# A hybrid layer on one Trainium2 core: the second gate's product cut in two, its row spread through memory, and one expert's weights asked for first

## The chip, the cores and the metric

The kernel runs on one core of one Trainium2 chip. The metric is the device time of one launch in microseconds (us). Engines are TensorE (PE, products; PEld is its weight load), VectorE (DVE), ScalarE (ACT), GpSimd (POOL) and SyncE (SP, which here issues most transfers). Each engine works through its own instructions in order; semaphores tie them together. Sixteen DMA engines move the data between the memory of the chip (DRAM) and the on-chip buffers.

## The reference

One transformer layer for 256 tokens of width 1024, in float32. A conditioning vector c gives six modulation rows:

```
mod = (silu_c @ w_ada + b_ada).reshape(bsz, 6, d)
sh1, sc1, g1, sh2, sc2, g2 = ...
u = modulate(x, sh1, sc1)
mix = hybrid_mixer(u, ...)                 # RG-LRU half, attention half, w_out
x = layernorm(ALPHA * x + g1 * mix, ln1_g, ln1_b)
u2 = modulate(x, sh2, sc2)
ffn = hierarchical_moe(u2, ...)            # 32 experts, 2 per token, chosen by a router
x = layernorm(ALPHA * x + g2 * ffn, ln2_g, ln2_b)
```

The change touches the last of these rows, g2 (called v=5 in the kernel), which multiplies what the experts give.

## The kernel before, in words

The tokens are handled as two halves of 128 (i = 0 and 1). The kernel is one long straight program: a tile framework puts in the semaphores, but the order of the instructions on every engine is the order of the source (`manual_schedule`), so a line that stands earlier in the source is earlier on its engine.

The stages, in order: the modulation rows and the input projection (to about 100 us); attention, output product and first layer norm, together with the router, mixed by hand (100 to 165 us); then the experts (165 to 290 us) and the last layer norm.

Weights come in loads of 1024 KB, two per call of `load` (line 229), issued by SP. SP goes through its list in order; a load waits until the buffer that it overwrites is free. `arena` has six slots of 16 KB per partition; `last`, `misc` and `fifth` are three more buffers of that size. `last` takes the place of the buffers of the input projection; `misc` holds small things and the softmax tiles until `pv_mm(1, 1)`; `fifth` takes the place of `mT` and `lnb` when the second half's `x2_of` has read them.

Six experts are expected to be busy, from the router's bias alone. `early_experts` ranks them on DVE and leaves their row numbers in `eos`. `statics((e, part), ...)` (line 859) issues the loads of expert e: part 0 and 1 are w1 and w3 (into `place[e][0]`), part 2 is w2. The first call also makes SP read six numbers of `eos` into registers (line 856). Experts 0 to 3 are used by the first `products` (line 1212, `ph0`), experts 4 and 5 by later units. The other experts are only known when the router is done; `bring_all` loads them (lines 1166 and 1169) as the buffers come free.

Gate v of the modulation is a product over 1024 inputs in two halves: `V1[v, q]` holds the weights of half q, `vec_mm(v, q, pa2)` (line 590) makes 16 calls that add to the bank `pa2`. For g2 the bias rows are added by four small products, ACT copies the result to `row3` (four rows of 256, at partitions 0, 32, 64 and 96), and four products with a broadcast column of the identity spread it over all partitions into the bank `acc[1]`; ACT copies it to `g2b`. The first reader of `g2b` is line 1362, which scales the first experts' output rows.

The row for the second modulation already goes through DRAM: `mod2_out` writes `mod2d`, `mod2_in` reads it back as `mod2p` (SP, lines 660 and 664). `constants()` (lines 942 to 946) reads `mod2p[:, 1]`.

For token half i, `bn_end` (line 885) makes the mean and the reciprocal standard deviation: DVE adds epsilon (line 274), POOL takes the power -0.5 (line 275). `logits` needs that value in its second instruction (line 933); `top` picks the experts; then PE ranks the tokens (lines 1127 to 1131), DVE makes slots, and `early_rows(1)` on PE (line 1070) gathers the tokens for the early experts. `norms` (line 1050 on POOL, line 1051 on ACT) makes the rows that it gathers.

Of the kernel before, what the change touches and what calls it, by code (L numbers as in the profile page):

```python
# [10 lines left out]
F32 = mybir.dt.float32  # L11
# [4 lines left out]
AF = mybir.ActivationFunctionType  # L16
# [5 lines left out]
S, D = 256, 1024  # L22
# [125 lines left out]
def layer(ctx: ExitStack, tc: tile.TileContext, at_a, at_b, x, w_ada, b_ada, w_in, w_out, w1, w3, w2,  # L148
          pack_a, pack_b, w_gate, rb, ln, out, dbg=None):
    nc = tc.nc  # L150
    te, ve, se, ge, sy = nc.tensor, nc.vector, nc.scalar, nc.gpsimd, nc.sync
# [7 lines left out]
    drm = ctx.enter_context(tc.tile_pool(name="drm", bufs=1, space=DRAM))  # L159
# [15 lines left out]
    misc = front.enter_context(tc.tile_pool(name="mis", bufs=1, reuse_waits="tile")).tile([128, 4096], F32, name="misc")  # L175
# [18 lines left out]
    def bank(pool=None):  # L194
        turn[0] += 1
        return (pool or (psx, psp)[turn[0] % 2]).tile([128, 512], F32, name="b")

    def abank():
        return psa.tile([128, 512], F32, name="a")
# [6 lines left out]
    brows = misc[:, 2048:3072].rearrange("p (g n) -> p g n", g=2)  # L206

    def A(name):
        o, w = at_a[name]
        return pka[:, o:o + w]  # L210

    def K(name, rows=128):
        o, w = at_b[name]
        return pkb[:rows, o:o + w]
# [9 lines left out]
    def load(s, src):  # L224
        n, w = src.shape[1:]
        t = (slot(s) if isinstance(s, int) else s).rearrange("p (k n) -> p k n", k=n)
        for h in range(2):
            q = slice(h * n // 2, (h + 1) * n // 2)
            sy.dma_start(t[:, q], src[:, q])  # L229
        return t  # L230

    def load_vec(v, q, s):
        return load(s, ada[:, 4 * q:4 * q + 4, v * D:(v + 1) * D])
# [16 lines left out]
    V1 = {}  # L250
# [7 lines left out]
    ident = A("ident")  # L258
# [23 lines left out]
    cd = ch.tile([128, KD, 32], F32, name="cd")  # L282
# [94 lines left out]
    def vec_cols(v):  # L377
        pa = abank()
        for k in range(KD):
            for j in range(4):  # L380
                te.matmul(pa[32 * j:32 * j + 32, 0:256], cd[:, k], V1[v, k // 4][:, k % 4, j * 256:(j + 1) * 256],
                          start=(k == 0), stop=(k == KD - 1), skip_group_check=True, tile_position=(0, 32 * j))
        r = tmp.tile([128, 256], F32, name="row", bufs=1)
        ve.tensor_copy(r, pa[:, 0:256])
        p = bank(psx)
        for s in range(2):
            te.matmul(p[:, s:8:2], r[:, s * 128:(s + 1) * 128], sel4, start=True, stop=True)
        return p[:, 0:8]
# [69 lines left out]
    p = vec_cols(0)  # L458
# [20 lines left out]
    for k in range(KD):  # L479
        j = k % 4  # L480
        te.matmul(pb[32 * j:32 * j + 32], shd[:, k], W["x"][:, k], start=(k < 4), stop=(k >= 4), skip_group_check=True,  # L481
                  tile_position=(0, 32 * j))
# [57 lines left out]
    def early_experts():  # L540
        row, rank = prior[:, :NE], prior[:, NE:2 * NE]
        ve.tensor_scalar(stat, rank, RS - 0.5, 32.0, op0=OP.is_gt, op1=OP.mult)
        ve.scalar_tensor_tensor(stat, rank, RS + NS - 0.5, stat, op0=OP.is_lt, op1=OP.mult)
        ve.tensor_scalar(e32, rank, 32.0, -32.0 * RS - 128.0 * UA, op0=OP.mult, op1=OP.add)


        ve.tensor_scalar(row, rank, 0.5, 64.0, op0=OP.is_lt, op1=OP.mult)
        ve.tensor_add(cap, stat, row)
        ve.tensor_scalar(row, rank, 1.5, 64.0, op0=OP.is_lt, op1=OP.mult)
        ve.tensor_add(cap, cap, row)  # L550
        ve.scalar_tensor_tensor(row, rank, float(NS + 1), row, op0=OP.add, op1=OP.mult)
        ve.tensor_scalar(v512, rank, 2.0, 2.0 * (1 - RS), op0=OP.mult, op1=OP.add)
        ve.tensor_mul(v512, v512, stat)
        ve.tensor_add(v512, v512, row)
        ve.tensor_scalar(v512, v512, 8.0, None, op0=OP.mult)
        ve.tensor_scalar(sel[:, 3], cap, -1.0, None, op0=OP.mult)
        ve.tensor_copy(dat[:, :, 0], K("foff"))
        eid = ch.tile([128, NS + 2], F32, name="eids")
        for j in range(NS + 2):
            ve.scalar_tensor_tensor(row, rank, float(RS + j if j < NS else j - NS), K("e"), op0=OP.is_equal, op1=OP.mult,  # L560
                                    accum_out=eid[:, j:j + 1])
        ve.tensor_scalar(eos, eid, 128.0, None, op0=OP.mult)
# [23 lines left out]
    def vec_mm(v, q, pt):  # L586
        o = (v - 4) * 256
        for k in range(4):
            for j in range(4):
                te.matmul(pt[32 * j:32 * j + 32, o:o + 256], cd[:, 4 * q + k], V1[v, q][:, k, j * 256:(j + 1) * 256],  # L590
                          start=(q + k == 0), stop=(v == 4 and q == 1 and k == 3), skip_group_check=True,
                          tile_position=(0, 32 * j))

    def vec_rows(v, pt):
# [147 lines left out]
    def pt(i, b):  # L742
        sn, at = AT[i, b]
        n, w = sn.shape[1:]
        p = bank()
        for c in range(n):
            for j in range(w // 128):
                o = (j * n + c) * 128
                te.transpose(p[:, o:o + 128], sn[:, c, j * 128:(j + 1) * 128], ident)
        t = misc[:, 3072 + at:3584 + at]  # L750
        se.activation(t, p, AF.Copy)
        AT[i, b] = t
# [55 lines left out]
    def base(i, h):  # L808
        p = wo_mm(i, h, 0)
        sl = slice(h * 512, (h + 1) * 512)  # L810
        t = tmp.tile([128, 512], F32, name="s")
        ve.scalar_tensor_tensor(t, p, rl[:, i:i + 1], g1b[:, sl], op0=OP.mult, op1=OP.mult)
        ve.scalar_tensor_tensor(xt[:, i, sl], xt[:, i, sl], ALPHA, t, op0=OP.mult, op1=OP.add)
# [24 lines left out]
    early.close()  # L838
    late = ctx.enter_context(tc.tile_pool(name="lat", bufs=1, reuse_waits="tile"))
    last = late.tile([128, 4096], F32, name="last")  # L840
    V1[5, 1] = load_vec(5, 1, last)
    merge = ctx.enter_context(ExitStack())
    merge_pool = merge.enter_context(tc.tile_pool(name="mrg", bufs=1, reuse_waits="tile"))
    mT = merge_pool.tile([128, 8, 256], F32, name="mT")
# [4 lines left out]
    pa2 = abank()  # L849
# [4 lines left out]
    def load_static(e, part):  # L854
        if not srows:
            srows.extend(nc.values_load(eos[0:1, j:j + 1], engines=[mybir.EngineType.SP], min_val=0, max_val=(NE - 1) * 128)
                         for j in range(NS + 2))
        src = ex[("w1", "w3", "w2")[part]][bass.ds(srows[e], 128)]
        sy.dma_start(place[e][1] if part == 2 else place[e][0][:, part * 2048:(part + 1) * 2048], src)
# [3 lines left out]
    def statics(*parts):  # L863
        for e, part in parts:
            load_static(e, part)
# [51 lines left out]
    def raw_mm(i, zT):  # L917
        p = bank(psp)
        for k in range(KD):
            te.matmul(p[:, 0:36], zT[:, k], wsh[:, k, 0:36], start=(k == 0), stop=(k == KD - 1))  # L920
        return p
# [19 lines left out]
    def constants():  # L941
        ve.tensor_tensor(wsh[:, :, 36:72], wr, cols_of(mod2p[:, 1]), op=OP.mult)
        ve.tensor_tensor(wsh[:, :, 0:36], wsh[:, :, 36:72], cols_of(A("lcol")[:, 0:8]), op=OP.mult)
        ve.tensor_tensor(wsh[:, :, 72:108], wsh[:, :, 36:72], cols_of(A("lcol")[:, 8:16]), op=OP.mult)

        ve.tensor_reduce(wsum[:, 0:108], wsh.rearrange("p k e -> p e k"), axis=AX.X, op=OP.add)
# [37 lines left out]
    norm(0, 1)  # L984
    pt(0, 0)
    early_experts()
    vec_mm(4, 0, pa2)
    statics((0, 0), (0, 1))
    pt(0, 1)
# [25 lines left out]
    scores(1, 3)  # L1015
    constants()
    vec_mm(5, 0, pa2)
    statics((2, 0), (2, 1))
    pv_mm(1, 0)
    vec_mm(5, 1, pa2)  # L1020
    for j in range(4):
        te.matmul(pa2[32 * j:32 * j + 32, 256:512], ident[:, 32 * j:32 * j + 1].to_broadcast([128, 32]), brows[:, 1, 256:512],
                  start=False, stop=True, skip_group_check=True, tile_position=(0, 32 * j))
    row3 = cd.rearrange("p k n -> p (k n)")
    se.activation(row3, pa2[:, 256:512], AF.Copy)
    statics((3, 0), (3, 1))
    pt(1, 2)
    norm(1, 3)
    base(1, 0)
# [10 lines left out]
    logits(0, t0, st0)  # L1040
    top(0)
    base(1, 1)
    statics((4, 0), (4, 1), (0, 2), (1, 2))
    rms_cols(row, ra[:, 1:2], psp)
    bs = [wo_mm(1, 0, 1, psx)]
    nmr = ch.tile([128, 2], F32, name="nmr")
# [50 lines left out]
    acc = [[accp.tile([128, 512], F32, name=f"acc{i}{h}") for h in range(2)] for i in range(2)]  # L1097
# [3 lines left out]

    acc_init(0, 0)
    pl1 = raw_mm(1, zT1)
    g2b = mox.tile([128, D], F32, name="g2b")
    for j in range(4):
        te.matmul(acc[1][j // 2][:, j % 2 * 256:j % 2 * 256 + 256], ident[:, 32 * j:32 * j + 1].to_broadcast([128, 128]), row3,
                  start=True, stop=True)
    acc_init(0, 1)
    for h in range(2):
        se.activation(g2b[:, h * 512:(h + 1) * 512], acc[1][h], AF.Copy)  # L1110
    x2_of(1, *lnst[1])
    st1 = bn(1, x2[:, 1])
    st1 = bn_end(*st1)
# [2 lines left out]
    merge.close()  # L1116
    fifth = ctx.enter_context(tc.tile_pool(name="fif", bufs=1, reuse_waits="tile")).tile([128, 4096], F32, name="fifth")
    place.append((fifth, w2_at[5]))
    statics((4, 2), (5, 0), (5, 1), (5, 2))
    logits(1, t1, st1)  # L1120
    top(1)
    dump("lg", lg)
# [3 lines left out]
    p = bank(psp)  # L1126
# [66 lines left out]
    for k in range(KD):  # L1193
        q, sc, sh = pgs[k // 4][:, k % 4 * 128:k % 4 * 128 + 128], mod2p[:, 1, k:k + 1], mod2p[:, 0, k:k + 1]
# [541 lines left out]
```

## Time and profile before

| | |
|---|---|
| time, median of 3 runs | 307.26 us (307.08 to 308.35) |
| the profiled execution | 307.51 us, its span 305.7 us |
| PE busy | 278.0 us (91%) |
| DVE busy | 181.7 us (59%) |
| ACT busy | 108.2 us (35%) |
| POOL busy | 23.6 us (8%) |
| moved by the DMA engines | 112.22 MB, mean 367 GB/s |
| mean granted PE clock | 0.988 of full speed |

The span runs from the first to the last instruction of one execution; the time also holds what lies around it. Busy times are of one engine and overlap with those of the others. A chain of waits is followed back from the last instruction: at each step to what released it, or else to the instruction ahead of it on its engine. In rows, `L590` is line 590; `b<-arena,mT` reads "writes b, reads arena and mT"; `x32` counts instructions (one float32 product in the source is two of them).

### The profile page before, as it was taken

How to read it: one execution, taken by the hardware profiler on the slowest of the kernel's cores; microseconds unless marked ns; L12 is line 12 of the kernel's file. 1: busy time of each engine (PE TensorE's matmuls, PEld its weight loads, DVE VectorE, ACT ScalarE, POOL GpSimd, SP SyncE). 2: the span in 40 equal slices, each digit the busy share in tenths (PEclk: the TensorE clock that was granted, in tenths of full speed). 3: DMA queues.
4: the chain of work that ended last, by engine and by line, in shares of the span. 5: the costliest groups of instructions: out<-in, count | busy, mean ns of one | idle time of the engine just before them, and what ended most of it. 6: DMA issues, size and time to landing. Idle time of an engine off the chain costs nothing.

```text
span 305.7 us, 6096 instructions
## 1 busy us (share of the span) xinstructions
PE 278.0 (91%) x2344; PEld 185.1 (61%) x2344; DVE 181.7 (59%) x442; ACT 108.2 (35%) x229; POOL 23.6 (8%) x62
## 2 busy tenths in 40 slices
PE   0699889999999999999988969999999999998980
PEld 0579649797957745457475656667546754664430
DVE  2675167937686796689698964264426343434281
ACT  1233068868937542043417341113111312121110
POOL 0100613000010000000110200000000000400000
PEclk9999979999999999999999999999999999999997
DMA  7999999999999699699969999999999999999404
GB/s 271 387 391 408 393 396 404 385 395 420 411 409 407 248 416 421 235 402 378 323 263 364 364 416 427 418 421 419 423 423 415 421 419 420 421 414 404 177 3 148
DMA packets 26163, 112.22 MB, mean 367 GB/s; under 512 B 2253, under 2 KB 3586, under 8 KB 17420
## 3 DMA queue, kind: packets, MB, share of 16 engines
q1 hardware_dynamic: 25712, 111.26, 91.7%
q10 hardware_dynamic: 348, 0.47, 0.4%
q8 instruction: 20, 0.33, 0.4%
q14 instruction: 19, 0.16, 0.2%
q0 software_dynamic: 64, 0.01, 0.0%
HBM read 110.51 MB, written 1.22 MB: 365 GB/s over the span
## 4 chain that ended last, share of the span: by engine, by line
PE 63%; DMA 13%; DVE 12%; SPq 6%; ACT 2%; issue 2%; DVEq 0%; ACTq 0%
PE m L1212 14%; PE b L430 12%; PE m L1350 8%; PE b L804 7%; DMA arena<-in_w 6%; DMA arena<-in_w_in 6%; SPq L229 4%; PE b L779 4%; PE m L1288 4%; PE acc L1311 3%; PE a L578 2%; PE a L590 2%; PE acc L1387 1%; PE b L481 1%; PE b L617 1%
## 5 line engine op out<-in xcount | busy, mean ns | idle before, releaser
L430 PEld LDWEIGHTS b<-ul,w 128*128 128x128 f32 x384 | 46.6, 192 | 5.0 <-ACT ul L470 1.6
L430 PE MATMUL b<-ul,w 128*128 128x256 f32 x384 | 48.4, 286 | 0.5 <-ACT w L410 0.5
L1212 PE MATMUL m<-arena,xg 128*64 128x256 f32 (+1 forms) x288 | 36.1, 380 | 1.0 <-DMA arena<-in_w 1.0
L408 DVE TENSOR_TENSOR w<-arena,w 128x512 fp32r<-128x512 f32 x32 | 21.9, 700 | 16.1 <-ACT w L407 16.1
L1350 PE MATMUL m<-arena,hT 128*32 128x512 f32 (+2 forms) x184 | 29.1, 596 | 1.6 <-ACT hT L1341 1.6
L804 PE MATMUL b<-arena,mT 128*128 128x512 f32 x64 | 29.0, 601 | 0.0
L1212 PEld LDWEIGHTS m<-arena,xg 128*64 128x64 f32 (+1 forms) x288 | 21.1, 125 | 9.9 <-DMA arena<-in_w 1.7
L407 ACT ACTIVATE w<-arena 128x512 fp32r<-128x512 f32 x32 | 19.5, 625 | 13.9 <-DMA arena<-in_w_in 7.1
L1212 PE MATMUL m<-fifth,xg 128*32 128x256 f32 (+1 forms) x96 | 21.5, 380 | 0.0
L1212 PE MATMUL m<-misc,xg 128*32 128x256 f32 (+1 forms) x160 | 21.4, 380 | 0.0
L1362 DVE SCALAR_TENSOR_TENSOR ys<-m,ws,g2b 128x256 f32<-128x256 f32 (+1 forms) x21 | 11.4, 570 | 16.0 <-PE m L1350 15.8
L1363 ACT ACTIVATE yh<-ys 128x256 fp32r<-128x256 f32 (+1 forms) x21 | 10.0, 488 | 27.0 <-DVE ys L1362 26.9
L1331 DVE TENSOR_TENSOR hh<-hh,m 128x256 f32<-128x256 f32 x7 | 3.0, 422 | 27.9 <-ACT hh L1330 27.9
L804 PEld LDWEIGHTS b<-arena,mT 128*128 128x128 f32 x64 | 11.6, 191 | 13.0 <-issue 12.7
L1350 PEld LDWEIGHTS m<-arena,hT 128*32 128x32 f32 (+2 forms) x184 | 8.6, 120 | 17.8 <-issue 12.7
L1330 ACT ACTIVATE hh<-m 128x256 f32<-128x256 f32 x7 | 2.7, 385 | 41.1 <-PE m L1212 41.1
L1288 PE MATMUL m<-oh,xb 128*128 128x256 f32 (+1 forms) x64 | 15.4, 281 | 1.3 <-DVE oh L1279 1.3
L1288 PE MATMUL m<-oh,xa 128*128 128x256 f32 (+1 forms) x64 | 15.4, 282 | 0.0
L1212 PEld LDWEIGHTS m<-misc,xg 128*32 128x32 f32 (+1 forms) x160 | 13.3, 126 | 1.6 <-issue 0.8
L1212 PE MATMUL m<-last,xg 128*32 128x256 f32 x64 | 14.2, 380 | 0.0
L728 ACT ACTIVATE s<-s,z 128x128 f32<-128x128 f32 (+1 forms) x16 | 7.1, 449 | 18.3 <-DVE z L726 18.3
L305 PE MATMUL b<-pka,nx 128*128 128x128 f32 x16 | 3.9, 428 | 10.3 <-DVE nx L303 10.3
(321 smaller groups left out, 501.2 us busy)
## 6 DMA issues: line engine op xcount, KB each, us to landing
arena<-in_w SPq DMA_DIRECT2D x41, 1024.0 KB, 11.9
arena<-in_w_ada SPq DMA_DIRECT2D x22, 1024.0 KB, 13.9
arena<-in_w_in SPq DMA_DIRECT2D x10, 1024.0 KB, 15.1
last<-in_w SPq DMA_DIRECT2D x6, 1024.0 KB, 12.2
misc<-in_w SPq DMA_DIRECT2D x6, 1024.0 KB, 13.3
fifth<-in_w SPq DMA_DIRECT2D x6, 1024.0 KB, 13.0
arena<-in_w_out SPq DMA_DIRECT2D x4, 1024.0 KB, 8.8
arena<-in_w SPq DMA_DIRECT2D x8, 512.0 KB, 12.7
```

The costliest lines, as they stand in the source:

```text
L229: sy.dma_start(t[:, q], src[:, q])
L407: se.activation(t[:, 0], w[:, k], AF.Copy)
L408: ve.tensor_sub(t[:, 1], w[:, k], t[:, 0])
L430: te.matmul(half(bs, m), t[:, a, m * 128:(m + 1) * 128], ul[:, b, k], start=(k + m % 2 + a + b == 0), stop=(k == KD - 1 and a == 1), skip_ ...
L779: te.matmul(pvv[i], ul[:, ua, k, i * 128:(i + 1) * 128], t[:, wa], start=(k + wa + ua == 0), stop=(k == KD - 1 and wa == 1))
L804: te.matmul(p, mT[:, k, i * 128:(i + 1) * 128], wo[k // 4][:, k % 4, h * 512:(h + 1) * 512], start=(m == 0), stop=(m == 3))
L1212: te.matmul(ph[o:o + w, a * 256:(a + 1) * 256], xs[:, k, o:o + w], place[q][0].rearrange("p (a k f) -> p a k f", a=2, k=KD)[:, a, k], star ...
L1288: te.matmul(q, nhl[i][:, a, k * 128:(k + 1) * 128], oh[:, i, :n], start=(a + i == 0), stop=(a + i == 2))
L1311: te.matmul(acc[i][h], G[:, i * 128:(i + 1) * 128], y[:, sl], start=False, stop=False, skip_group_check=True)
L1350: te.matmul(ps[h][o:o + w], hT[:, j, o:o + w], place[q][1][:, j * 1024 + h * 512:j * 1024 + (h + 1) * 512], start=(j == 0), stop=(j == 1), ...
L1362: ve.scalar_tensor_tensor(ys[:, o:o + q], p[:, o:o + q], ws, g2b[:, sl], op0=OP.mult, op1=OP.mult)
L1363: se.activation(yh[:, sl], ys[:, o:o + q], AF.Copy)
```

## The change

The edits:

- The loads of `V1[5, 1]` no longer go into `last` behind `V1[5, 0]`; they go into `misc`, behind `statics((2, 0), (2, 1))`, in the place of `statics((4, 0), (4, 1))`.
- `statics((3, 0), (3, 1))` (into `last`) is the first call of `statics`, so these are the first loads of experts; `(4, 0), (4, 1)` come behind `(5, 0), (5, 1)`.
- `vec_mm(5, 1, pa2)` moves behind `raw_mm(1, zT1)`, the router's products for the second half. The bias rows stay, behind `vec_mm(5, 0)`.
- The four broadcast products and two ACT copies of `g2b` go. Instead POOL writes the four rows to a DRAM tile `g2d` and reads them back, 4 KB to each of 128 partitions, into `g2b`.

```diff
@@ in vec_mm @@
-                          start=(q + k == 0), stop=(v == 4 and q == 1 and k == 3), skip_group_check=True,
+                          start=(q + k == 0), stop=(q == 1 and k == 3), skip_group_check=True,
@@ behind early.close() @@
     last = late.tile([128, 4096], F32, name="last")
-    V1[5, 1] = load_vec(5, 1, last)
...
     early_experts()
+    statics((3, 0), (3, 1))
     vec_mm(4, 0, pa2)
...
     vec_mm(5, 0, pa2)
+    for j in range(4):
+        te.matmul(pa2[32 * j:32 * j + 32, 256:512], ident[:, 32 * j:32 * j + 1].to_broadcast([128, 32]), brows[:, 1, 256:512],
+                  start=False, stop=False, skip_group_check=True, tile_position=(0, 32 * j))
     statics((2, 0), (2, 1))
     pv_mm(1, 0)
-    vec_mm(5, 1, pa2)
-    for j in range(4):
-        te.matmul(pa2[32 * j:32 * j + 32, 256:512], ident[:, 32 * j:32 * j + 1].to_broadcast([128, 32]), brows[:, 1, 256:512],
-                  start=False, stop=True, skip_group_check=True, tile_position=(0, 32 * j))
-    row3 = cd.rearrange("p k n -> p (k n)")
-    se.activation(row3, pa2[:, 256:512], AF.Copy)
-    statics((3, 0), (3, 1))
     pt(1, 2)
...
     base(1, 1)
-    statics((4, 0), (4, 1), (0, 2), (1, 2))
+    V1[5, 1] = load_vec(5, 1, misc)
+    statics((0, 2), (1, 2))
...
     acc_init(0, 0)
     pl1 = raw_mm(1, zT1)
+
+    vec_mm(5, 1, pa2)
+    row3 = cd.rearrange("p k n -> p (k n)")
+    se.activation(row3, pa2[:, 256:512], AF.Copy)
+    g2d = drm.tile([4, 256], F32, name="g2d")
+    ge.dma_start(g2d, row3[0:128:32])
     g2b = mox.tile([128, D], F32, name="g2b")
-    for j in range(4):
-        te.matmul(acc[1][j // 2][:, j % 2 * 256:j % 2 * 256 + 256], ident[:, 32 * j:32 * j + 1].to_broadcast([128, 128]), row3,
-                  start=True, stop=True)
+    ge.dma_start(g2b, bass.AP(tensor=g2d.tensor, offset=g2d.offset, ap=[[0, 128], [1, D]]))
     acc_init(0, 1)
-    for h in range(2):
-        se.activation(g2b[:, h * 512:(h + 1) * 512], acc[1][h], AF.Copy)
     x2_of(1, *lnst[1])
     st1 = bn(1, x2[:, 1])
     st1 = bn_end(*st1)
     t1 = raw_end(1, pl1, lnst[1])
     norms(1, *st1)
     merge.close()
...
-    statics((4, 2), (5, 0), (5, 1), (5, 2))
+    statics((5, 0), (5, 1), (4, 0), (4, 1), (4, 2), (5, 2))
     logits(1, t1, st1)
```

## Rows read from the trace of the kernel before

**Rows 1.** PE, longest waits from 90 us on; columns: us in total, times, longest

```profile
PE m L1350 <- ACT hT L1341: 1.6, 3, 1.1
...
PE m L1212 <- DMA arena<-in_w: 1.0, 1, 1.0
```

**Rows 2.** The chain that ended last, in order of time; columns: start, us, what

```profile
130.33 1.86 PE a L590 x32
...
149.77 0.76 DVE s L895
...
157.12 1.41 DVE xt L905 x2
...
161.00 0.27 DVE lg L933
```

**Rows 3.** The same chain, near its end

```profile
257.28 19.75 DMA arena<-in_w
```

**Rows 4.** Windows; engines' busy time, granted PE clock, DMA share, GB/s

```profile
101.92:104.92 3.00, 3.00 (x31) 2.14 (x34) 1.37 (x7) 2.30 (x7) 0.71 (x1) 1.00 0.60 187
124.00:132.00 8.00, 8.00 (x89) 4.05 (x91) 6.45 (x12) 0.00 (x0) 0.54 (x1) 1.00 0.61 222
175.00:280.00 105.00, 101.06 (x891) 63.09 (x892) 49.11 (x123) 23.68 (x53) 3.18 (x4) 1.00 1.01 420
```

**Rows 5.** PE's timeline, 137 to 165 us

```profile
137.35 0.60 PE L749 MATMUL b<-pka,misc 128*128 128x128 f32 x4
...
159.75 1.97 PE L1106 MATMUL acc<-cd,pka 128*128 128x256 f32 x8
...
163.57 1.96 PE L1100 MATMUL acc<-xt,aid 128*128 128x512 f32 x4
```

**Rows 6.** ACT's timeline, two single lines

```profile
134.04 0.39 ACT L1025 ACTIVATE cd<-a 128x256 f32<-128x256 f32 x1
...
165.64 0.36 ACTq L1189 DMA_DIRECT2D keptd<-keepers  x1
```

**Rows 7.** DVE's timeline, 132 to 136 us

```profile
132.16 0.45 DVE L942 TENSOR_TENSOR arena<-pkb,mod2p 128x288 f32<-128x288 f32 x1
...
135.33 0.69 DVE L739 TENSOR_TENSOR misc<-s,z 128x512 f32<-128x512 f32 x1
```

**Rows 8.** SP's timeline, the DMA issues; columns: start, us, engine, line, what

```profile
101.92 0.90 SPq L229 DMA_DIRECT2D arena<-in_w_ada  x2
...
113.45 0.93 SPq L859 DMA_DIRECT2D arena<-in_w  x2
...
123.01 0.33 SPq L664 DMA_DIRECT2D mod2p<-mod2d  x1
...
171.20 2.23 SPq L1166 DMA_DIRECT2D arena<-in_w  x3
```

**Rows 9.** SP's waits, 84 to 180 us

```profile
SPq L664 <- DMA mod2d<-misc: 16.3, 2, 10.3
```

**Rows 10.** DMA issues by line: count, size, median us from issue to landing

```profile
out<-arena SPq DMA_DIRECT2D x4, 256.0 KB, 3.3
...
mod2p<-mod2d SPq DMA_DIRECT2D x2, 4.0 KB, 5.6
```

**Rows 11.** POOL's timeline, 155 to 175 us

```profile
160.24 0.55 POOL L275 TENSOR_TENSOR brs<-brs,negh 128x1 f32<-128x1 f32 x1 [3.29 <-DVE brs L274]
```

**Rows 12.** Instructions that write or read the tile lnr

```profile
L1373 POOL DMA_DIRECT2D lnr<-in_ln x2: 547/714/882, 171.0 to 171.9; - x2
...
DMA to landing us min/median/max: 5.6/5.7/5.8
```

**Rows 13.** Packets of ACT's DMA queue, 169 to 173 us: number, MB, share

```profile
q10 hardware_dynamic: 144, 0.15, 10.4%
```

**Rows 14.** Windows of PE alone: busy, granted clock, DMA share, GB/s

```profile
37.60:39.10 1.50, 0.16 (x2) 1.00 1.01 400
39.10:42.70 3.60, 3.58 (x17) 0.53 1.05 391
```

## Prediction, made before the changed kernel was run

> **What bounds the kernel now.** I read the waits of TensorE (PE) first. From 90 us on they are short: the list begins with 1.6 us in three waits, and only one wait is for a weight, 1.0 us for an expert's matrix [rows 1]. Then the chain in order of time [rows 2]: PE products up to 149 us; then VectorE (DVE), which normalises and routes the second 128 tokens, from 149.77 us on; then the experts' products, with one step at 257.28 that runs through a transfer for 19.75 us [rows 3]. Last the windows [rows 4]: from 175 to 280 us PE is busy 101 of 105 us and the DMA engines move 420 GB/s at a share of 1.01. So the last 105 us are full on both sides. Nothing after 175 us can absorb a delay, and an earlier start pays only if PE and the weight stream both start earlier.
>
> **The change part by part.** First what leaves PE. The second half product of gate v=5 (16 calls, the step from 130.33 to 132.19) is 1.86 us of the PE chain [rows 2]; it goes to where the four broadcast products of line 1106 stood, at 159.75, 1.97 us by their row, part of it overlapped [rows 5], so that place stays about as long as it was. The bias rows only move up a few products. Two ACT copies at line 1110 become one of 0.39 us, priced by line 1025 [rows 6]; ACT waits there anyway.
>
> Not all of the 1.86 us arrives. After the gap is closed PE would reach pt(1,3) at 137.35 - 1.86 = 135.5, but its input, norm(1,3), runs on DVE at 135.33 for 0.69 [rows 5, 7], which ends at 136.0. That leaves 1.2 us of gain. It shrinks further by the queue. One 1024 KB load at 420 GB/s takes 2.5 us, and a queue that starts again loses 3 x (1 - 187/420) = 1.66 us after its issue [rows 4, 8]. Before, five loads are issued from 101.92 on, and they cover the time until SyncE (SP), having read the expert numbers, issues the first expert load at 113.45. After the change three are: V1[5,0] and the layer norm rows, done at 101.92 + 1.66 + 7.5 = 111.1. The next bytes, now the fourth early expert's, come at 113.45 + 1.66 = 115.1; asking first cannot make SP read the expert numbers sooner. So mod2d, the small write that SP waits for, stands behind four loads from 115.1 (125.1) where it stood behind seven from 103.6 (121.1; SP woke at 123.01 [rows 8, 9], 1.9 later). SP wakes at 127.0. Its read back, mod2p, landed 5.6 us after 123.01 [rows 10], 2.5 after the nine loads ahead of it were through (126.1); now it lands at 115.1 + 15.0 + 2.5 = 132.6. constants() reads it on DVE at 132.16 [rows 7]: a wait of 0 to 0.5 us that the queue used to hide. I take the gain on PE as 1.0 us (bounds 0.7 and 1.2).
>
> The moved V1[5,1] itself is covered: it can be asked for when pt(1,3) has read its buffer, at about 137, with nothing left ahead of it in the queue (six loads from 115.1 and two more end at 135.1), and its reader comes at 158.8. The expert loads that it pushes back, (4,0) and (4,1), are first read in the unit after the early four. If it were late, PE would stand before its product, in front of everything that routes.
>
> Now what is new on GpSimd (POOL). The row of the gate goes through DRAM: POOL issues the write g2d, then the read g2b, which needs g2d landed. Both stand in program order ahead of the POOL steps of the second token half: the power that makes its standard deviation (line 275, at 160.24 for 0.55) [rows 11], then nmr. Line 933 on DVE, at 161.00 in the chain, needs that power [rows 2]; the routing, the rank products on PE, early_rows(1), the first expert products and the release of the first buffers all need line 933. An engine waits where it issues: SP's instruction behind mod2d did not start until it had landed, 16.3 us in two waits [rows 9]. I expect the same of POOL.
>
> The Trainium skill, DMA: Bandwidth & Descriptors, section "Two DMAs through the same engine are not ordered", says that only the completion semaphore orders a read behind a write, and that the issuing engine has to wait on it before it issues the second. By that rule the sum below stands; without a held POOL the sum is that of rival 2, 309.8 us. No row here shows POOL in such a wait.
>
> How long. Product ends: 159.75 - 1.0 + 1.86 = 160.6; ACT starts 0.2 later and takes 0.39: 161.2; POOL issues g2d at 161.3. Its landing is the large unknown. The nearest row is POOL's only other transfer, lnr: 4 KB, landed 5.6 to 5.8 us after issue [rows 12]. The low end is the output's store to DRAM, 3.3 us with the queue otherwise empty [rows 10]. The high end is ACT's write to DRAM keptd, issued at 165.64 beside loaded queues: all its packets lie in 169 to 173 us [rows 6, 13], so about 7.9 us with the receipt. I take 5.7, by the row of the same engine: landed at 167.0. Then g2b is issued, 0.1 + 0.71 by lnr's issue [rows 12] (g2b has 128 rows, not 2, so it may be longer by some us, not shorter): 167.8. Then the power, 0.05 + 0.55: 168.4, and line 933 some 0.2 later, at 168.6 where it was at 161.00. That is **+7.6 us**.
>
> The Trainium skill, DMA: Bandwidth & Descriptors, section "Anatomy of one DMA — SWDGE (gpsimd) path", gives about 2.0 us of fixed cost for such a transfer. By that figure the total would be 3.7 us lower, 312.8; it is no end of my range, and the lnr rows speak against it.
>
> While DVE stands, PE has acc_init(0,1) and one rank product, done by 161.6, and stands until 163.47 + 7.6 = 171.1: 9.5 us without work. The nearest row for that: at 37.60 to 39.10 PE did 0.16 us of work, and from 39.10 to 42.70 its granted clock was 0.53, near the lower of its two levels (1.2 of 2.4 GHz), then 1.00 [rows 14]. That is 3.6 x (1 - 0.53) = 1.7 us lost. After the stall that falls on acc_init(1) (1.96 us at 163.57 [rows 5]) and early_rows(1), both on the path. I take **+1.7** (bounds 0, if the clock holds, and 1.7).
>
> Sum: 7.6 + 1.7 = 9.3 us for everything from the rank products on. The first loads of the remaining experts are issued at 171.20 [rows 8], when PE releases the first buffers; they shift by the same 9.3, and the DMA queue runs empty before that (its six loads and g2b end at 175.4, below), so the stream shifts as PE does and the 1.0 us wait at 277 stays. Profiled execution 307.51 (span 305.7) + 9.3 = 316.8; that execution is 0.25 above the median of the runs shown, so 316.5 us on that scale. g2b itself is first read by the first experts' output rows, behind two whole sets of products, and lands under these.
>
> **The rivals.** Rival 1, same place, shorter: g2d lands after 3.3 us. Line 933 moves by 5.2 us: 312.5 without a clock loss, 314.1 with it. For it: DVE and PE are idle then. Against it: lnr's 5.7.
>
> Rival 2, POOL is not held, or not on the path; then the stream decides. The fifth buffer is free when DVE ends line 905 (158.53 [rows 2]) less 1.0; plus 1.66, 159.2; then six loads, 15.0 us, and g2b's half MB, 1.25 us: 175.4. Before, the loads behind these were issued at 171.20 [rows 8] and ran from 172.9 at the latest. So the last 105 us of the stream start some 2.5 us later: 309.8 us. For it: the full DMA share to 280 us. Against it: POOL's program order.
>
> Rival 3, the other side: faster. It needs POOL past g2b by 160.2, the time at which the power ran, and no later stream; PE then starts 1.0 to 1.4 us earlier and waits less at 277: 306.1 us. For it: PE is on the chain from 130 to 149 us, and 124 to 132 us, at 222 GB/s [rows 4], leaves 3.8 us of transfer time that earlier loads can fill. Against it: a write that is not issued before 161.3 cannot have landed by 160.2, and the hole from 111 to 115 us opens instead.
>
> **How the numbers follow.** A measurement of this kernel can tell about 0.5% (1.5 us) from no change. Chances: the forecast, with g2d landing in 4.5 to 8 us, 0.68; rival 1, 0.12; rival 2, 0.09; rival 3, 0.06; longer than 8 us or a long g2b issue, 0.05. The long landing gives 7.6 + 2.2 + 1.7 = 11.5 us, 318.7, and 1 us more for g2b's issue 319.7. The range 310.8 to 319.7 holds the forecast and rival 1, 0.80. Slower: forecast, rival 1, the long tail and two thirds of rival 2, 0.91; within 0.5%: 0.04; faster: 0.05.
>
> **What would show it.** Right: on POOL's timeline the read g2b starts some 5 to 6 us after the write, the power of the second half (line 275) comes after it near 168, DVE shows one wait of about 8 us at line 933, PE one of about 9 us before line 1128 with a lower granted clock behind it, and the DMA windows near 176 to 181 us are thin. The hole at 111 to 115 us and the constants() wait near 132 show the queue steps. Wrong: the power at about 159 us, before g2b; a g2d that lands within 3 us; or PE waiting for V1[5,1].

## The result, and the profile after

The changed kernel takes 316.85 us (median of 4 runs, 316.07 to 317.27); the kernel before takes 307.81 us on the same chip (307.08 to 308.60). The ratio is 1.0286, with a 95% interval of 1.0249 to 1.0324: slower by 9.0 us, where 9.3 were forecast. The profiled execution's span is 314.8 us (305.7 before), its mean granted PE clock 0.979 (0.988).

One difference between the two executions lies ahead of every edit. In the one before, PE's clock was at half from 39.1 to 42.7 us [rows 14]; in the one after it was at 1.00, and the 16 products of line 481 that run there took about half as long. First PE before, then PE after and its window (columns as in [rows 4]):

```profile
39.12 3.60 PE L481 MATMUL b<-arena,misc 128*32 128x512 f32 x16 [1.35 <-DVE misc L467]
```

```profile
39.53 1.92 PE L481 MATMUL b<-arena,misc 128*32 128x512 f32 x16 [0.68 <-DVE misc L467]
```

```profile
39.00:42.80 3.80, 3.27 (x27) 1.83 (x28) 3.39 (x9) 3.62 (x7) 1.78 (x5) 1.00 1.04 389
```

So what PE paces runs early in the trace after, by 1.22 us: the constants on DVE start at 130.94 where they stood at 132.16 [rows 7]. Below, "on the common start" means that 1.22 is added to a time of after. Kernels are compared so wherever their start clocks differ.

The first view is POOL's timeline after, in the stretch of [rows 11]; in brackets is the idle time before an instruction and what ended it:

```profile
160.34 0.90 POOL L1106 DMA_DIRECT2D g2d<-cd  x1 [5.59 <-ACT cd L1104]
166.24 0.60 POOL L1108 DMA_DIRECT2D g2b<-g2d  x1 [5.00 <-DMA g2d<-cd]
166.85 0.56 POOL L275 TENSOR_TENSOR brs<-brs,negh 128x1 f32<-128x1 f32 x1
167.52 0.32 POOL L1047 TENSOR_SCALAR nmr<-bmv,brs 128x1 f32<-128x1 f32 x1
```

The read of g2b stands 5.00 us for its own write, and the power comes only behind it. The waits of DVE, then of PE, after (total, times, longest) show who stands behind the power (the edits move line numbers by one or more: line 932 after is line 933 before):

```profile
DVE lg L932 <- POOL brs L275: 8.7, 1, 8.7
```

```profile
PE b L1127 <- DVE mb L981: 9.3, 1, 9.3
```

The chain that ended last, in order of time, answers to [rows 2, 3]: the landing of g2d is now on it, the two groups of PE behind it are long, and near the end the weights' transfer follows as before.

```profile
160.34 5.59 DMA g2d<-cd
...
166.85 0.57 POOL brs L275
...
167.45 0.27 DVE lg L932
...
170.19 3.60 PE acc L1097 x4
173.79 1.64 PE b L1067 x8
...
175.53 1.36 DVE xt L1197 x4
...
265.75 19.80 DMA arena<-in_w
285.59 7.15 PE m L1211 x122
```

The windows after, with columns as in [rows 4], show the rest: the hole at 111 to 115 us (131 GB/s), 124 to 132 us filled (379 GB/s where it was 222), PE at half clock from 165 to 175 us, and the stream nearly dry at 174 to 182 us (67 GB/s), because nothing frees a buffer.

```profile
111.00:115.00 4.00, 3.75 (x49) 2.35 (x50) 3.33 (x7) 2.97 (x11) 0.55 (x1) 1.00 0.42 131
124.00:132.00 8.00, 7.78 (x71) 4.01 (x70) 6.58 (x14) 0.95 (x4) 0.54 (x1) 1.00 1.00 379
165.00:175.00 10.00, 5.08 (x15) 3.02 (x15) 5.31 (x27) 4.61 (x9) 1.48 (x3) 0.50 0.98 401
174.00:182.00 8.00, 8.00 (x123) 5.65 (x126) 6.13 (x21) 2.70 (x7) 1.72 (x3) 0.92 0.24 67
```

SP's timeline after, beside [rows 8]: the first expert loads at 112.63, mod2p asked for at 125.26, V1[5,1] (misc) at 135.59, the loads of the remaining experts at 179.91 instead of 171.20.

```profile
112.63 0.93 SPq L858 DMA_DIRECT2D last<-in_w  x2
...
125.26 0.33 SPq L664 DMA_DIRECT2D mod2p<-mod2d  x1
...
135.59 2.51 SPq L229 DMA_DIRECT2D misc<-in_w_ada  x2
...
179.91 1.63 SPq L1165 DMA_DIRECT2D arena<-in_w  x3
```

### The profile page after: what moved, and what is told of

It is laid out like the page before. It is cut to its first block, busy times and chain, and to the rows that moved or that the text cites. A ratio compares the mean times of both kernels' runs of the same rounds, so it can differ in the third digit from the quotient of the medians.

```text
span 314.8 us, 6081 instructions
## 1 busy us (share of the span) xinstructions
PE 278.8 (89%) x2336; PEld 185.6 (59%) x2336; DVE 182.1 (58%) x442; ACT 107.5 (34%) x227; POOL 25.8 (8%) x64
## 3 DMA queue, kind: packets, MB, share of 16 engines
HBM read 111.04 MB, written 1.22 MB: 357 GB/s over the span
## 4 chain that ended last, share of the span: by engine, by line
PE 63%; DMA 16%; DVE 13%; ACT 3%; issue 2%; POOL 1%; DVEq 0%; ACTq 0%
PE m L1211 13%; PE b L430 11%; PE m L1349 7%; DMA arena<-in_w 6%; DMA arena<-in_w_in 6%; PE b L804 6%; PE b L779 4%; PE m L1287 4%; PE acc L1310 3%; PE a L578 2%; DMA g2d<-cd 2%; DMA pka<-in_pack_a 2%; PE acc L1097 2%; PE b L1067 1%; PE acc L1386 1%
## 5 line engine op out<-in xcount | busy, mean ns | idle before, releaser
L408 DVE TENSOR_TENSOR w<-arena,w 128x512 fp32r<-128x512 f32 x32 | 21.9, 699 | 13.9 <-ACT w L407 13.9
L1211 PEld LDWEIGHTS m<-fifth,xg 128*32 128x32 f32 (+1 forms) x96 | 11.1, 119 | 3.5 <-DMA arena<-in_w 0.8
## 6 DMA issues: line engine op xcount, KB each, us to landing
arena<-in_w SPq DMA_DIRECT2D x41, 1024.0 KB, 12.1
arena<-in_w_ada SPq DMA_DIRECT2D x22, 1024.0 KB, 13.9
last<-in_w SPq DMA_DIRECT2D x6, 1024.0 KB, 12.1
```

Source lines behind the costliest of these rows:

```text
L408: ve.tensor_sub(t[:, 1], w[:, k], t[:, 0])
L1211: te.matmul(ph[o:o + w, a * 256:(a + 1) * 256], xs[:, k, o:o + w], place[q][0].rearrange("p (a k f) -> p a k f", a=2, k=KD)[:, a, k], star ...
```

## Experiments

The theory: POOL, held by its own read, delays the power, and PE, standing meanwhile, comes back at half clock. The rivals: the transfer itself is late for another reason (who issues it), or the weight stream, not POOL, sets the end.

**The trip behind the power.** In the changed kernel, both transfers move behind `norms(1, *st1)`.

```
     acc_init(0, 1)
...
     norms(1, *st1)
+    g2d = drm.tile([4, 256], F32, name="g2d")
+    ge.dma_start(g2d, row3[0:128:32])
+    g2b = mox.tile([128, D], F32, name="g2b")
+    ge.dma_start(g2b, bass.AP(tensor=g2d.tensor, offset=g2d.offset, ap=[[0, 128], [1, D]]))
```

> The changed kernel with both g2 transfers moved behind norms(1) on GpSimd, all else as changed. Theory (the place in GpSimd's queue is the cost): the power of the second half runs near 159 us again, the 8.7 us wait of VectorE at its logits and the low clock behind it are gone, and what is left is the later weight stream: 308 to 310 us. Rival A (the moved product, its weights and the order of the loads cost most of it): 313 us or more. Rival B (the change is a gain of about 1 us on TensorE once GpSimd is free): 306 us.

Measured: 313.10 us, ratio 1.0166 (1.0122 to 1.0209); the span is 311.4. The power runs at 159.48 and line 932 at 160.24, 0.76 earlier than before at the same start clock. POOL still stands 5.2 us for g2d, now with nothing behind it that the second half's routing needs. So POOL's hold was real and is gone, yet 4.7 us remain: the forecast of 308 to 310 us is missed, and the time is that of rival A. The timeline of PE in this kernel shows where: two waits for weights near the end, and the last products slow.

```profile
278.55 1.06 PE L1211 MATMUL m<-arena,xg 128*32 128x256 f32 x2 [3.27 <-DMA arena<-in_w]
281.04 0.63 PE L1211 MATMUL m<-arena,xg 128*32 128x256 f32 x1 [1.42 <-DMA arena<-in_w]
```

The chain and a window of the same kernel, and the same step of the chain before:

```profile
281.04 9.04 PE m L1211 x122
```

```profile
281.00:285.00 4.00, 3.96 (x40) 1.87 (x44) 0.00 (x0) 0.00 (x0) 0.00 (x0) 0.50 1.03 407
```

```profile
277.07 7.09 PE m L1212 x122
```

The last weights come 281.04 - 277.07 = 3.97 us later than before, and their products lose 9.04 - 7.09 = 1.95 us to the half clock. The weight stream is a second cost, which POOL's hold had covered.

**The trip alone.** The kernel before, with the four broadcast products and two copies replaced by the two transfers, in the same place; product and loads stay.

```
+    g2d = drm.tile([4, 256], F32, name="g2d")
+    ge.dma_start(g2d, row3[0:128:32])
     g2b = mox.tile([128, D], F32, name="g2b")
-    for j in range(4):
-        te.matmul(acc[1][j // 2][:, j % 2 * 256:j % 2 * 256 + 256], ident[:, 32 * j:32 * j + 1].to_broadcast([128, 128]), row3,
-                  start=True, stop=True)
+    ge.dma_start(g2b, bass.AP(tensor=g2d.tensor, offset=g2d.offset, ap=[[0, 128], [1, D]]))
     acc_init(0, 1)
-    for h in range(2):
-        se.activation(g2b[:, h * 512:(h + 1) * 512], acc[1][h], AF.Copy)
```

> The kernel before with only the row's way through memory in the place of the four products and the two ScalarE copies; the half product stays early. Theory: GpSimd issues the write at about 157 us (behind the first power of that half), it lands 5.6 us later, the read takes 0.6, so the second power ends near 164.0 where it ended at 160.8: 3.2 us late; TensorE stands some 6 us, so the lower clock adds up to 1.7: 310.5 to 312.5 us. Rival (what costs is the half MB in the weight stream, not the wait): 1.3 us, 308.8 us at most.

Measured: 310.99 us, ratio 1.0097 (1.0062 to 1.0133). The row is ready early, so the write is issued at 157.25, behind the first half's power, and lands 3.8 us later, not 5.6. This is from the view of the tile g2d, of this kernel:

```profile
DMA to landing us min/median/max: 3.8/6.4/9.1
```

The same line of the changed kernel (the first figure is g2d, the last g2b):

```profile
DMA to landing us min/median/max: 5.6/7.2/8.9
```

The queue differs at the time of each write: 209 GB/s here (157.2 to 161.1), 421 after.

```profile
157.20:161.10 3.90, 3.69 (x21) 2.64 (x22) 3.76 (x10) 0.16 (x1) 0.95 (x2) 1.00 0.50 209
```

```profile
160.30:165.90 5.60, 0.35 (x2) 0.10 (x1) 0.00 (x0) 0.00 (x0) 0.90 (x1) 0.92 1.01 421
```

Line 933 is 1.59 us later than before (162.59 against 161.00), PE stands 3.9 us, and from line 933 to `xt`, the first input of the experts, it takes 170.12 - 162.59 = 7.53 us where before took 167.06 - 161.00 = 6.06: the clock costs 1.47 us after that short stand too. The total lies in its forecast, but not by its terms: a landing of 5.6 us and a power 3.2 us late were forecast, 3.8 and 1.6 came.

POOL's other transfer of 4 KB, lnr (a read from DRAM, 5.6 to 5.8 us before [rows 12]), is in every kernel and bears out that the landing goes with the traffic. In the changed kernel its two halves are issued at 179.46 and 180.09, while the stream starts again after its dry stretch (129 GB/s over the first landing, 298 over the second). In the changed kernel with the ranking early (below) the stream starts again still later, with 39 and 267 GB/s. The tile lnr in the one and in the other:

```profile
DMA to landing us min/median/max: 2.9/3.9/5.0
```

```profile
DMA to landing us min/median/max: 1.8/3.1/4.4
```

**The write issued by ACT.** One word of the changed kernel: `se.dma_start(g2d, ...)` instead of `ge.dma_start`.

> The changed kernel with the write of the row issued by ScalarE right behind its own copy; the read stays on GpSimd at its place. Theory (GpSimd waits for the landing, whoever issued the write, and the landing is slow because the DMA engines are full): a landing of 5 to 7 us, 316 to 318 us. Rival (GpSimd's own way of issuing is slow, and a write from another queue lands in about 3.3 us): 313.5 to 314.5 us.

Measured: 316.23 us, ratio 1.0270 (1.0213 to 1.0327), as the changed kernel. ACT's write starts at 161.3, and POOL's read again starts 6.0 us later:

```profile
167.26 0.86 POOL L1108 DMA_DIRECT2D g2b<-g2d  x1 [11.25 <-DMA g2d<-cd]
```

So the issuing engine is not what makes the landing long.

**Products that keep PE busy.** The changed kernel, with 8 and then 10 products of 128x512 ahead of the rank products that wait (their bank is overwritten later). The diff is of the first; the second has `range(5)`.

```
+    for n in range(4):
+        for h in range(2):
+            te.matmul(acc[1][h], aid, x2[:, 0, h * 512:(h + 1) * 512], start=True, stop=True)
```

> The changed kernel with eight extra 128x512 products into the bank that is written afresh afterwards, ahead of the first rank product that waits: some 7 us of work in a 9.3 us wait, their results are not used. Theory (1.7 to 2 us of the loss is the lower clock behind the wait): granted clock 1.00 throughout, 314.6 to 315.4 us. Rival (the clock behind the wait is beside the path): 316.9 us, or more by what the products delay.

> The changed kernel with ten extra products (some 8.8 us) where the shorter filler had eight, so that TensorE stands for about 0.6 us before the rank products in place of 2.4. Their results are not used. Theory (the lower clock behind the wait is worth 1.7 to 2 us on the path): granted clock 1.00 through the rank products and early_rows(1), which take 1.8 and 2.0 us again; 2 us below the changed kernel, a ratio to the kernel before near 1.021. Rival (the products behind the wait are slow for another reason, or are beside the path): the ratio of the changed kernel, 1.027 to 1.029.

Measured: 315.50 us with 8 products, ratio 1.0224 (1.0169 to 1.0278), and 314.95 with 10, 1.0219 (1.0135 to 1.0303). The medians are lower than the changed kernel's, by intervals that overlap with its own; the traces are clearer. With 8, PE still stood 2.4 us and its clock fell after 170 us, where 1.00 throughout was forecast; with 10 it stood 0.74 and the clock stayed at 1.00. PE's timeline with 10:

```profile
161.85 8.75 PE L1128 MATMUL acc<-xt,aid 128*128 128x512 f32 x20
...
171.46 1.96 PE L1097 MATMUL acc<-xt,aid 128*128 128x512 f32 x4
173.26 1.97 PE L1067 MATMUL b<-wsd,nx 128*128 128x128 f32 x16
```

and the changed kernel's, without:

```profile
170.03 3.76 PE L1097 MATMUL acc<-xt,aid 128*128 128x512 f32 x4
173.58 2.73 PE L1067 MATMUL b<-wsd,nx 128*128 128x128 f32 x16
```

From line 932 to `xt` it takes 174.96 - 168.90 = 6.06 us with 10 products, 7.20 with 8, and 175.53 - 167.45 = 8.08 in the changed kernel, against 6.06 before. The stand costs 2.02 us through the clock, and work on PE alone gives all of it back. Against the kernel before, whose clock at 39 us was at half like that of the kernel with 10 products, `xt` starts 174.96 - 167.06 = 7.90 us later, where the changed kernel's starts 9.69 later on the common start.

**The hole at 111 to 115 us.** The ranking of the experts, on DVE, moves out of `early_experts` to a place behind `scores(0, 0)`. It is then done some 13 us earlier, and SP issues the first expert load some 4.5 us earlier (108.08 against 112.56 us in the two kernels without the trip, below). It was done in the changed kernel, in the one with the trip behind the power, and in the kernel before as a control.

```
         ve.tensor_copy(dat[:, :, 0], K("foff"))
+
+
+    def early_ids():
+        row, rank = prior[:, :NE], prior[:, NE:2 * NE]
         eid = ch.tile([128, NS + 2], F32, name="eids")
...
     scores(0, 0)
+    early_ids()
```

> The changed kernel, with GpSimd's wait left in, and the expert numbers early as in the run beside it. Theory (the two costs lie side by side: the stream's 4 us are hidden behind the 9 us by which the path is late): the hole at 111 to 115 us closes and the time stays within 1 us of the changed kernel, ratio 1.024 to 1.030. Rival (the costs add): 4 us less, ratio 1.014 to 1.016.

> Both g2 transfers behind norms(1), and the seven instructions that give SyncE the expert numbers moved from early_experts to behind scores(0, 0) on VectorE, into a gap of 2.2 us there. Theory (what is left without GpSimd's wait is the later weight stream, most of it the hole at 111 to 116 us, in which SyncE has not yet read the expert numbers): the hole of 4.4 us closes, no wait for a weight of over 1 us on TensorE near 280 us, 306 to 308.5 us (ratio 0.993 to 1.002). Rival (the half MB of g2b and the later holes cost the 4 us): 311 us or more.

> Control: the kernel before with the expert numbers early. Its queue is covered until 116 us by V1[5, 1], so the first expert loads only join the queue sooner. Theory: no change, ratio 0.995 to 1.003. Rival (the early numbers are a gain by themselves): 2 us or more faster.

Measured: 317.08 us in the changed kernel, ratio 1.0281 (1.0217 to 1.0345), no gain, though the stream runs at 428 GB/s from 111 to 116 us. With the trip behind the power 311.94, 1.0141 (1.0085 to 1.0198), 1.2 us less than without this edit, intervals overlapping: 306 to 308.5 was forecast, and the rival's 311 or more came. In the kernel before 308.13, 1.0001 (0.9966 to 1.0035), no change. The hole that I had made the stream's main loss is a small part of it.

**Order and transfer apart.** Three kernels without the trip. In the first both transfers are left out and g2b is set to 1.0; the second spreads the row by PE again; the third is the first with the ranking early. The diff is of the first; the second has the four broadcast products and two copies of the kernel before behind `acc_init(0, 1)` instead of the last two lines.

```
-    g2d = drm.tile([4, 256], F32, name="g2d")
-    ge.dma_start(g2d, row3[0:128:32])
-    g2b = mox.tile([128, D], F32, name="g2b")
-    ge.dma_start(g2b, bass.AP(tensor=g2d.tensor, offset=g2d.offset, ap=[[0, 128], [1, D]]))
     acc_init(0, 1)
...
     norms(1, *st1)
+    g2b = mox.tile([128, D], F32, name="g2b")
+    ge.memset(g2b, 1.0)
```

> The changed kernel without the trip through memory: both transfers of g2d and g2b are left out, and g2b is set to 1.0 by POOL behind norms(1), so the gate of the last modulation is missing from the output; the new place of the half product and the new order of the loads stay. Theory: two costs lie side by side in the changed kernel, the trip ahead of POOL's power and a weight stream that is about 3.8 us late without it. Of these 3.8 us, 1.25 are g2b's half MB and some 2.5 the holes that the new order of the loads opens. So this kernel has no wait of POOL and DVE, PE starts the first products some 1.0 us earlier than in the kernel before, and the stream is still 2.5 us late: waits for weights of 2 to 4 us in sum near 277 us, 309.8 us without a fall of the clock there and up to 311.5 with one. Rival: the order of the loads costs nothing at the end and the half MB is the whole delay: 306.5 to 308.5, faster or the same.

> The changed kernel with the row of g2 spread by PE again: behind acc_init(0,1), four broadcast products into acc[1] and two copies on ACT, as in the kernel before, in the place of the two transfers. Theory: the same as without the trip, as the stream sets the end: 310 to 312 us; the four products (1.97 us by their row of before) fall partly into the 0.9 us in which PE stands before the rank products, so PE gives its 1.0 us back, and the waits for weights get shorter by about as much. Rival: PE decides, not the stream: the 1.0 us lost on PE shows as well, 1 us above the run without the trip.

> The run without the trip (both transfers left out, g2b set to 1.0) and the ranking of the experts moved behind scores(0,0), so that SP has their numbers some 5 us earlier and the hole in the stream from 111 to 115 us closes. Theory: other holes, at 133 to 137 us above all, take its place, as in the run with the trip behind the norms, which this edit brought 1.2 us: 308.5 to 310.5 us, still slower than the kernel before. Rival: the hole at 111 to 115 is what makes the stream late: then this kernel is as fast as the one before or up to 1.0 us faster, 306 to 308.

Measured: 310.73 us without the trip, ratio 1.0113 (1.0050 to 1.0175); 309.88 with the row spread by PE, 1.0061 (1.0024 to 1.0097), a little under its forecast; 309.85 with the ranking early, 1.0079 (1.0038 to 1.0119). None is as fast as the kernel before, though POOL waits for no transfer in any of them: what they share, the moved half product and the new order of the loads, costs time. It isn't the product: with the ranking early PE reaches the rank products at 160.48 without the trip and at 161.43 in the kernel before, so PE is ahead there, and the order is what is left. The row spread by PE shows no cost against no row at all, so the rival in which PE decides finds nothing for it.

Three kernels with the ranking early, all with the start clock at 1.00, take the stream apart. PE's last weights: the kernel before with the ranking early, then the new order without the trip, then the new order with the trip behind the power.

```profile
274.89 0.40 PE L1216 MATMUL m<-arena,xg 128*32 128x256 f32 x1 [0.89 <-DMA arena<-in_w]
```

```profile
276.81 0.64 PE L1213 MATMUL m<-arena,xg 128*32 128x256 f32 x1 [1.83 <-DMA arena<-in_w]
```

```profile
278.96 0.63 PE L1215 MATMUL m<-arena,xg 128*32 128x256 f32 x1 [1.86 <-DMA arena<-in_w]
```

The order costs 276.81 - 274.89 = 1.92 us, the trip another 2.15; its half MB at 420 GB/s is 1.25 of these. Over 100 to 182 us the DMA engines also move less with the trip, 345 GB/s against 349, which is another 0.8 us; most of it is lost at 168 to 176 us (397 against 422 GB/s, at a DMA share of 1.01 against 1.03). What is lost by the order can be seen at 131 to 139 us. First the kernel before, ranking early, then the new order without the trip:

```profile
131.00:134.00 3.00, 3.00 (x9) 1.34 (x8) 2.91 (x5) 1.87 (x7) 0.00 (x0) 1.00 1.00 423
134.00:139.00 5.00, 5.00 (x46) 4.32 (x44) 4.32 (x7) 2.57 (x7) 0.00 (x0) 1.00 1.00 383
```

```profile
131.00:134.00 3.00, 2.87 (x13) 1.60 (x11) 2.93 (x6) 2.10 (x8) 0.00 (x0) 1.00 0.67 284
134.00:139.00 5.00, 4.80 (x46) 4.20 (x50) 4.97 (x8) 2.15 (x7) 0.00 (x0) 1.00 0.63 210
```

The loads into `last` go out at 108.08 instead of 129.35, and nothing is left to ask for until `misc` is free at 134.75. At 420 GB/s the second pair of windows loses 3.5 us, the first 0.4; smaller holes later are fewer in the new order, and over 100 to 182 us the loss grows from 12.1 us (358 GB/s) to 13.9 (349), by 1.8, which is most of the 1.92.

## Why the prediction was right, point by point

- **PE's gain, 1.0 us: right.** The moved product starts at 157.64, where the broadcast products stood at 159.75 [rows 5]: 2.11, less the 1.22 of the start, 0.9 us. pt(1,3) starts at 134.86, just behind its input (norm(1,3) at 134.12 for 0.69), as forecast.
- **The queue steps: the place right, the size too large.** The hole at 111 to 115 us is there, with 4 x (1 - 131/420) = 2.75 us lost where all 4.0 were forecast. SP woke at 125.26, 126.48 on the common start (forecast 127.0), and mod2p was in time for the constants at 130.94: the forecast 0 to 0.5 us came out as none. V1[5,1] was in time.
- **POOL held, +7.6 us: right.** On the common start the write is issued at 161.56 (forecast 161.3), lands after 5.6 (5.7, from lnr), and line 932 starts at 167.45 + 1.22 = 168.67, 7.67 us later than before. The issue of g2b took 0.60 (0.71, which I had called a lower end). With the trip moved, the wait at line 932 was gone, and the same read's wait cost POOL nothing that anyone waited for: this is shown, not only argued. The Trainium skill, DMA: Bandwidth & Descriptors, section "Two DMAs through the same engine are not ordered", asks for that wait between the two; the trace agrees (5.00 us). The figure of about 2.0 us that the same page of the Trainium skill gives, in section "Anatomy of one DMA — SWDGE (gpsimd) path", fits no landing of g2d: 3.8 us with the queue half busy, 5.6 with it full. Only lnr comes near it, with 1.8 us at 39 GB/s.
- **The clock, +1.7 us: right in kind, a little small.** It cost 2.02: from line 932 to `xt` 8.08 us against 6.06; the 10 filling products bring it back to 6.06.
- **The sum, 9.3 us: right.** `xt` starts 175.53 + 1.22 - 167.06 = 9.69 us later on the common start (7.67 + 2.02), the last weights' products 8.52 + 1.22 = 9.74. The 1.0 us wait near the end stayed (1.03). So the terms measured come to 9.7, 0.4 more than forecast. That the medians differ by 9.0 is nearer than the terms deserve, and in part luck: the spans of the two traces differ by 9.1, but by 10.3 on the common start, of which 0.6 lies behind the last weights (29.2 us from there to the end, 28.6 before), where no run explains it.
- **Rival 1** (a landing of 3.3 us) came near only where the queue was half empty. **Rival 3** (faster) did not come.
- **Rival 2 was a real second cost, and mis-sized.** Without POOL's hold I gave 309.8 us; the run gave 313.1. The stream was 3.97 us late instead of 2.5, and I had not counted that PE, standing for those weights, loses 1.95 us of clock once more. In the changed kernel this is hidden under POOL's hold, so the forecast did not feel it; as the worth of undoing the hold it was wrong: 316.5 - 309.8 = 6.7 us should have come back, 316.85 - 313.10 = 3.75 did.

What stays open: of the trip's 2.15 us in the stream, 0.9 is not bytes; some 0.8 shows as a lower rate, most of it while g2b is under way, and why the rate is lower no run shows. No run varied the traffic alone, so that it makes the landing long rests on the rows of g2d and lnr side by side.

## What to carry to other kernels

A read that must wait for a write holds everything behind it on the engine that issues it (here POOL, as SP before it): before sending a row through memory, list what stands behind the second transfer, and price the landing by a transfer of the same kind with the queue as full as it will be. A stand of PE can cost twice, the wait and then the clock (here behind 9.3, 3.9 and 2.4 us before the rank products, not behind 0.74), and filling work gives back only the second. A load asked for earlier leaves a hole where it used to stand, unless another buffer is free then.

## What the runs showed of the hardware

- A 4 KB transfer issued by POOL landed in 1.8 us with the DMA engines at 39 GB/s, 2.9 at 129, 3.8 at 209, 5.0 at 298 and 5.6 at 421 (lnr, a read, but for the 209 and the 421 of g2d, a write). With the write issued by ACT, POOL's read began 6.0 us after it, at 425 GB/s.
- The clock's fall near the end went with how PE's waits lay. Two waits of 1.24 and 1.89 us, with 0.62 us of products between them, were followed by products of 8.78 us at a clock of 0.59 from 277 to 281 us (the kernel without the trip); a single wait of 1.89 us, with PE busy before it, by 7.09 at 1.00 (the row spread by PE). These are the waits of the one and of the other:

```profile
275.08 0.62 PE L1209 MATMUL m<-arena,xg 128*32 128x256 f32 x2 [1.24 <-DMA arena<-in_w]
277.59 0.55 PE L1209 MATMUL m<-arena,xg 128*32 128x256 f32 x1 [1.89 <-DMA arena<-in_w]
```

```profile
279.06 0.40 PE L1213 MATMUL m<-arena,xg 128*32 128x256 f32 x1 [1.89 <-DMA arena<-in_w]
```

  The other traces agree: the three more with two waits there have 8.61 to 9.49 us for these products, those with one wait 7.09 to 7.15.

- The half clock at 39 to 43 us came in some profiled executions and not in others (0.55 before, 1.00 after, with the same program up to there), and shifts what PE paces by more than 1 us (1.22 at the constants). Two traces have to be set to a common start before terms of 1 us are read from them.
